# A hybrid recurrent block in fp32 on one core: preparations and inverse moved some input blocks ahead, the recurrence spread over more blocks

## The chip, the core and the metric

The kernel runs on one core of a Trainium2 chip. The metric is the device time of one execution in microseconds (us), as the median of several runs. A core has five engines with instruction queues of their own: TensorE (PE, matrix products), VectorE (DVE), ScalarE (ACT), GpSimd (POOL) and SyncE (SP, which here issues transfers). Each engine works through its queue in order and waits on semaphores for the others.

## The reference

One block over 512 positions of width 1024, batch 1, all in float32:

```python
h = rms_norm(x, norm_mix_g)
proj = h @ w_in + b_in                       # 1024 -> 4864 columns
y_a = rwkv7_branch(proj[:, :1792], ...) @ w_branch_a
y_b = rglru_branch(proj[:, 1792:2304], proj[:, 2304:2816], ...) @ w_branch_b
merged = sigmoid(proj[:, 2816:3840]) * y_a + sigmoid(proj[:, 3840:]) * y_b
x = x + merged @ w_mix_out
x = x + cross_attention(rms_norm(x), rms_norm(mem), w_cq, w_ckv, w_co)
x = x + conv_ffn(rms_norm(x), w_ffn_in, ffn_conv_w, ffn_conv_b, w_ffn_out)
out = rms_norm(x, norm_final_g)
# rwkv7_branch: r, k, v and two low-rank gates are shifted mixes of proj; per head (8 heads of 64) and position
#   sa = S a;  S = S diag(decay) + sa b^T + v k^T;  y = S r
#   then a group norm per head, a bonus sum(r k r_k) v, and a gate
# rglru_branch: xb = causal conv of 4 taps over px; gate_a, gate_x = sigmoid(block products of xb)
#   a = exp(8 gate_a log_sigmoid(lam)); u = xb gate_x sqrt(1 - a^2); h_t = a_t h_(t-1) + u_t; times gelu(py)
```

## The kernel before

**Products.** Channels lie on partitions and positions along the free axis. Each float32 operand is split into a high part (a cast on ACT, `win_h`) and a low part (a subtraction on DVE, `win_l`), and a product is the sum of three: high by high, low by high, high by low. The input projection runs in 38 blocks of 128 output columns. Block i is the PSUM tile `in_ps{i}`; it takes 48 matmuls of 128x256. Blocks 4 to 7 are k, 0 to 3 are r, 8 to 11 are v, 12 and 13 the low-rank inputs, 22 to 37 the merge gates, 14 to 17 px and 18 to 21 py. Weights are loaded by SP through four buffers and split into three pairs of buffers, so that the split of the block number g in `IN_ORDER` needs the end of the block that stands three before it. Three PSUM banks take the blocks' results.

**RWKV-7.** The recurrence is done in 8 chunks of 64 positions. For each pair j of heads come, once its k, r and v blocks are there:

- `prep(j)`: two low-rank products, `psw{j}` and `psa{j}`, and the decays;
- `prep2(j)`: the norm of kk by the product `ss{j}`, and the scaled operands `KBt` (both of its kinds, from kk and from k) and `AK`;
- `scores(j)`: the products `sc{j}`, masked by DVE and ACT into `AK` and `BZ`;
- `bonus_terms(j)`; the bonus products `bo{j}` follow later, DVE multiplies them into `bs{j}`.

Then each chunk's triangular matrix has to be inverted. The 32x32 diagonal blocks go through DRAM (`dM`) into `Nm`, with one block per partition. DVE runs 31 steps of growing size, each a multiplication into `zz` and a reduction into `Zt`, then copies to `Zn`; the result goes back through DRAM (`dZt`, `dZ`) into `ZA` and `BZ`, where products of 32x32, `zh0`, `zo0`, `zh16`, `zo16`, finish the off-diagonal blocks.

Chunk c of the recurrence: `x{c}` (8 products), copied by DVE into `Xs`; `y{c}`, first half; `u{c}` from Xs, copied by ACT and DVE into `UV`; `vr{c+1}`, the next rows of v; `s{c}` from UV; `y{c}`, second half; `kbr{c+1}`, transposes. From s DVE makes `Sn{c}`, then two parts of UV for the next chunk, then two of `SP{c}`. So the chain x, Xs, u, UV, s, Sn, UV, x runs back and forth between PE and DVE.

**RG-LRU.** `px_gates(b)` takes block 14+b: ACT makes `xb{b}`, DVE adds three shifted rows (128x511, 510, 509) and corrects three columns, PE makes `ga{b}` and `gx{b}` from xb. `px_scan(b)` works on pairs of b: exponentials and logarithms on ACT, and on DVE a scan into YB. xb has two buffers, so xb2 takes xb0's, once the scan of xb0 is done. `group_norm(0, jp, ...)` makes `gv0_jp` and `gg0_jp`, in the one PSUM bank that ga0 and gx0 and the like use too.

**Order.** Instructions on DVE, ACT and SP are ordered by the scheduler of the language, by the program's text and priorities. On PE the text table `ORDER` rules: `name` takes all that is left of a tile's products, `name:n` the next n; `Products.arrange` ties each product to the one before it. The other engines' order then follows from what the scheduler expects to be ready. `NSUM` counts, for the sums of squares ahead, how many are made at each block.

Of the kernel before, what the change touches and what calls it, by code (L numbers as in the profile page):

```python
# [41 lines left out]
ORDER = """
in_ps4 in_ps5 in_ps0 in_ps1 in_ps8 in_ps9 psw0 psa0 ss0 in_ps6 in_ps7 in_ps2:6 sc0 in_ps2:12 psw1 psa1 in_ps2:18
ss1 in_ps2 in_ps3 in_ps10:30 sc1 in_ps10 in_ps11 psw2 psa2 ss2 in_ps22 in_ps23 in_ps24:6 sc2 in_ps24 psw3 psa3
ss3 in_ps25 in_ps26 in_ps27:30 sc3 in_ps27 in_ps28 bo0 in_ps29 bo1 in_ps30 bo2 in_ps31 bo3 in_ps32 in_ps33
in_ps34 in_ps35 in_ps36 in_ps37 in_ps14 in_ps15:42 ga0 in_ps15 in_ps16:2 gx0 in_ps16:38 ga1 in_ps16:6 zh0 gx1
in_ps16 in_ps17:4 zo0 zh16 in_ps17:10 zo16 in_ps17:10 vr0 in_ps17:6 x0 y0:8 kbr0 in_ps17:2 u0 vr1 in_ps17:6 s0
y0 kbr1 in_ps17:4 x1 y1:8 in_ps17:2 u1 vr2 in_ps17 s1 y1 kbr2 in_ps18:8 x2 y2:8 in_ps18:4 u2 vr3 s2 y2 kbr3 ga2
in_ps18:2 x3 y3:8 gx2 u3 vr4 s3 y3 kbr4 ga3 x4 y4:8 u4 vr5 gx3 s4 y4 kbr5 in_ps18:6 x5 y5:8 u5 vr6 in_ps18:6 s5
y5 kbr6 in_ps18:2 x6 y6:8 vr7 in_ps18:2 u6 in_ps18:10 s6 y6 kbr7 in_ps18 gv0_0:1 in_ps19:8 x7 y7:8 in_ps19:6 u7  # L50
in_ps19:6 gv0_0 y7 in_ps19:4 gg0_0 in_ps19:20 gv0_1 in_ps19 in_ps20:16 gg0_1 in_ps20 in_ps21 gv1_0 gg1_0 gg1_1
yb_ps0:18 yb_ps1:10 gv1_1 yb_ps1:8 yb_ps0 yb_ps1 yb_ps2 yb_ps3 yb_ps4 yb_ps5 yb_ps6 yb_ps7 ya_ps0 ya_ps1 ya_ps2
ya_ps3 ya_ps4 ya_ps5 ya_ps6 ya_ps7 mix_ps0 mix_ps1 mix_ps2 mix_ps3 mix_ps4 mix_ps5 mix_ps6 mix_ps7 q_ps0_0:32
rxc_ps q_ps0_0 q_ps0_1 q_ps1_0:24 sc_ps0_0 sc_ps0_1 q_ps1_0 q_ps1_1:4 sc_ps0_2 prT_ps0:2 q_ps1_1:8 sc_ps0_3
prT_ps0:2 q_ps1_1:18 prT_ps0 q_ps1_1:10 o_ps0 q_ps1_1 o_ps1 q_ps2_0:4 sc_ps1_0 sc_ps1_1 q_ps2_0:16 sc_ps1_2
prT_ps1:2 sc_ps1_3 prT_ps1:2 q_ps2_0:16 prT_ps1 q_ps2_0:10 o_ps2 q_ps2_0 q_ps2_1:18 o_ps3 q_ps2_1 q_ps3_0:16
sc_ps2_0 sc_ps2_1 q_ps3_0:14 sc_ps2_2 prT_ps2:2 sc_ps2_3 prT_ps2:2 q_ps3_0:16 prT_ps2 q_ps3_0 q_ps3_1:16 o_ps4
q_ps3_1:16 o_ps5 q_ps3_1 co_ps0:16 sc_ps3_0 sc_ps3_1 co_ps0:14 sc_ps3_2 prT_ps3:2 sc_ps3_3 prT_ps3:2 co_ps0:6
co_ps4:10 prT_ps3 co_ps4:10 o_ps6 co_ps4:12 o_ps7 co_ps4:4 co_ps0:6 co_ps4:6 co_ps0 co_ps4 co_ps1
""".split()  # L60


# [17 lines left out]
def hybrid_block_kernel(ctx: ExitStack, tc: tile.TileContext, xT_d, mT_d, pv_d, cst_d, win_d, wk_d, wv_d,  # L80
                        lup_d, gup_d, rga_d, rgx_d, wba_d, wbb_d, wmix_d, wq_d, wo_d, wfi_d, wfo_d, out_d):
    nc = tc.nc
    V, S = nc.vector, nc.scalar
# [76 lines left out]
    def stream(dram, name, between=None, order=None, at=0):  # L160

        for g in order or range(dram.shape[0]):
            with tc.high_priority():
# [9 lines left out]
                wdma.append(ins)
                hi, lo = weight_tiles(name, g, at)
                for o in range(0, 1024, n):
                    casts.append(S.copy(hi[:, o:o + n], raw[:, o:o + n]))  # L176
                    V.tensor_tensor(lo[:, o:o + n], raw[:, o:o + n], hi[:, o:o + n].bitcast(F32), ALU.subtract)  # L177
# [466 lines left out]

    def inproj(i):
        nonlocal last_in
        ps = mm_ps(f"in_ps{i}")
        last_in = dense(ps, uin, lambda kb: (h2[:, 0, kb, :], h2[:, 1, kb, :]), KB, NSUM.get(i, 0))
        return ps

    def evac_shift(ps, blk, out):
# [3 lines left out]
        V.scalar_tensor_tensor(out, ps, omu[:, blk:blk + 1], q, ALU.mult, ALU.add)  # L655
# [113 lines left out]
    for jp in range(2):
        js = (2 * jp, 2 * jp + 1)  # L770
        pks, prs = {}, {}
        for j in js:
            pks[j] = pp.tile([P, T], F32, tag="pk", name=f"pk{j}", bufs=2)
            evac_shift(inproj(4 + j), 4 + j, pks[j])
        for j in js:
            prs[j] = pp.tile([P, T], F32, tag="pr", name=f"pr{j}", bufs=3)
            evac_shift(inproj(j), j, prs[j])
        for j in js:
            evac_shift(inproj(8 + j), 8 + j, vT[:, j, :])
        for j in js:  # L780
            if j == 3:
                for i in IN_REST[:NEARLY]:
                    gate_block(i - 22)
            at, L, Pp = prep(j)
            prep2(j, pks[j], prs[j], at, L, Pp)
            scores(j)
            bonus_terms(j, pks[j], prs[j])
# [838 lines left out]
```

## Time and profile before

| | |
|---|---|
| median of 3 runs | 879.01 us (878.78 to 880.6) |
| the profiled execution | 879.42 us, of which the span of the page is 877.6 |
| PE busy | 855.6 us, 97% of the span |
| DVE, ACT, POOL busy | 679.5, 514.0, 132.5 us |
| mean granted clock of PE | 0.998 |

A page gives the busy time of each engine, and for a group of instructions also the idle time of the engine just before them and what ended it. Since matmuls are pipelined, a matmul's own duration is longer than the distance to the next; delays are best read from starts. The projection blocks end at about 330 us; the preparations lie in 75 to 190, the inverse in 190 to 250, the recurrence in 275 to 330, the group norms and the first products of the branches up to 350.

### The profile page before, as it was taken

The page shows a single profiled execution, that of the slowest core. Times are in us where ns is not written, and L with a number is a line of the kernel's source. Part 1 is how long each engine was busy: PE and PEld are TensorE (multiplying, and loading weights), DVE is VectorE, ACT ScalarE, POOL GpSimd, SP SyncE. Part 2 cuts the span into 40 slices and gives each one's busy share as a digit, 9 for nine tenths or more (in the row PEclk, how much of TensorE's full clock was granted, in tenths as well). Part 3 has the DMA queues.
Part 4 walks back from the last instruction along what each step waited for, and adds up shares of the span by engine and source line. Part 5 has one row for each costly group of instructions (what it writes and reads, how often), then busy time and mean ns, then how long its engine had stood idle before and what let it go on. Part 6 is the DMA issues. An engine that isn't in the chain of part 4 may idle for free.

```text
span 877.6 us, 19313 instructions
## 1 busy us (share of the span) xinstructions
PE 855.6 (97%) x7884; PEld 825.9 (94%) x7884; DVE 679.5 (77%) x1096; ACT 514.0 (59%) x788; POOL 132.5 (15%) x163
## 2 busy tenths in 40 slices
PE   9999989999999999999999999999999999999996
PEld 8889989999997789999999899999999999999996
DVE  6796598877967686685575568799888888999774
ACT  7575676743437687234454356666666566867563
POOL 0102223021101022001122211102111121111100
PEclk9999999999999999999999999999999999999999
DMA  8888799777895479858987858999999999998953
GB/s 284 298 263 220 202 229 232 202 198 242 241 259 138 73 169 265 219 172 223 235 232 168 207 148 201 248 274 276 298 263 293 293 266 305 262 295 212 304 183 96
DMA packets 97576, 201.60 MB, mean 230 GB/s; under 512 B 19600, under 2 KB 30992, under 8 KB 97424
## 3 DMA queue, kind: packets, MB, share of 16 engines
q1 hardware_dynamic: 62240, 118.57, 40.2%
q0 software_dynamic: 25504, 67.38, 37.6%
q10 hardware_dynamic: 9744, 14.42, 4.9%
q8 instruction: 62, 1.02, 0.5%
q14 instruction: 26, 0.21, 0.1%
HBM read 188.54 MB, written 78.12 MB: 304 GB/s over the span
## 4 chain that ended last, share of the span: by engine, by line
PE 74%; DVE 13%; ACT 5%; DMA 4%; issue 3%; DVEq 0%; ACTq 0%; SPq 0%
PE fx_ps L95 14%; PE in_ps L95 13%; PE fyz_ps L95 10%; PE ox_ps L95 7%; PE oyz_ps L95 5%; PE co_ps L95 5%; PE mix_ps L95 4%; PE q_ps L95 4%; PE yb_ps L95 2%; DVE win_l L177 2%; PE v_ps L95 2%; PE o_ps L95 1%; PE k_ps L95 1%; DVE Zt L821 1%; DVE zz L820 1%
## 5 line engine op out<-in xcount | busy, mean ns | idle before, releaser
L95 PE MATMUL in_ps<-hT,win_h 128*128 128x256 f32 x1216 | 214.8, 280 | 2.1 <-DVE pr L655 1.6
L95 PEld LDWEIGHTS in_ps<-hT,win_h 128*128 128x128 f32 x1216 | 185.1, 188 | 6.1 <-DVE pr L655 1.8
L95 PE MATMUL in_ps<-hT,win_l 128*128 128x256 f32 x608 | 170.2, 280 | 1.1 <-DVE win_l L177 1.1
L199 ACT CAST wfi_h<-wfi_r 128x1024 fp32r<-128x1024 f32 x77 | 80.9, 1051 | 69.7 <-PE fyz_ps L95 25.2
L95 PEld LDWEIGHTS in_ps<-hT,win_l 128*128 128x128 f32 x608 | 114.2, 188 | 3.2 <-DVE win_l L177 1.7
L551 POOL DMA_DIRECT2D dS<-in_wfi x66 | 66.8, 1032 | 304.3 <-PE in_ps L95 127.5
L200 DVE TENSOR_TENSOR wfi_l<-wfi_r,wfi_h 128x1024 fp32r<-128x1024 f32 x77 | 94.1, 1222 | 19.8 <-ACT wfi_h L199 19.8
L177 DVE TENSOR_TENSOR win_l<-win_r,win_h 128x1024 fp32r<-128x1024 f32 x38 | 46.3, 1221 | 25.5 <-ACT win_h L176 25.2
L587 POOL DMA_DIRECT2D dOs<-in_wfo x54 | 39.9, 820 | 168.0 <-PE fx_ps L95 45.8
L95 PE MATMUL fx_ps<-hq,wfi_h 128*128 128x256 f32 x352 | 61.2, 276 | 0.0
L95 PE MATMUL fx_ps<-hr,wfi_h 128*128 128x256 f32 x352 | 61.1, 276 | 0.0
L95 PE MATMUL fyz_ps<-hq,wfi_h 128*128 128x256 f32 x352 | 61.1, 276 | 0.0
L95 PE MATMUL ox_ps<-go,wfo_h 128*128 128x256 f32 x352 | 59.9, 276 | 0.0
L176 ACT CAST win_h<-win_r 128x1024 fp32r<-128x1024 f32 x38 | 39.7, 1045 | 34.1 <-PE in_ps L95 31.1
L1436 DVE TENSOR_TENSOR wfo_l<-wfo_r,wfo_h 128x1024 fp32r<-128x1024 f32 (+1 forms) x39 | 47.2, 1213 | 11.6 <-ACT wfo_h L1435 11.6
L1435 ACT CAST wfo_h<-wfo_r 128x1024 fp32r<-128x1024 f32 (+1 forms) x39 | 40.4, 1036 | 25.1 <-DMA wfo_r<-dOs 8.2
L95 PEld LDWEIGHTS fx_ps<-hr,wfi_h 128*128 128x128 f32 x352 | 53.1, 188 | 0.2 <-ACT sn L1371 0.2
L95 PEld LDWEIGHTS fx_ps<-hq,wfi_h 128*128 128x128 f32 x352 | 53.2, 188 | 0.0
L95 PEld LDWEIGHTS fyz_ps<-hq,wfi_h 128*128 128x128 f32 x352 | 53.1, 188 | 0.0
L95 PEld LDWEIGHTS ox_ps<-go,wfo_h 128*128 128x128 f32 x352 | 52.9, 188 | 0.0
L95 PE MATMUL fyz_ps<-hq,wfi_l 128*128 128x256 f32 x176 | 48.7, 277 | 0.6 <-DVE wfi_l L200 0.6
L95 PE MATMUL fx_ps<-hq,wfi_l 128*128 128x256 f32 x176 | 48.6, 276 | 0.0
(392 smaller groups left out, 2337.0 us busy)
## 6 DMA issues: line engine op xcount, KB each, us to landing
dS<-in_wfi POOLq DMA_DIRECT2D x66, 512.0 KB, 8.3
wfi_r<-dS SPq DMA_DIRECT2D x44, 512.0 KB, 7.1
win_r<-in_win SPq DMA_DIRECT2D x38, 512.0 KB, 5.5
...
```

Of the source, the lines that this page charges most:

```text
L95: return self.log(out, nc.tensor.matmul(out, *args, **kw))
L176: casts.append(S.copy(hi[:, o:o + n], raw[:, o:o + n]))
L177: V.tensor_tensor(lo[:, o:o + n], raw[:, o:o + n], hi[:, o:o + n].bitcast(F32), ALU.subtract)
L199: S.copy(hi, raw)
L200: V.tensor_tensor(lo, raw, hi.bitcast(F32), ALU.subtract)
L551: return lambda: nc.gpsimd.dma_start(s(out), src, **kw)
L587: yield lambda k=k, w=w, src=src: nc.gpsimd.dma_start(dO[n, m][:, k * P:(k + w) * P], src, **kw)
L820: V.tensor_tensor(t3, Zt[:, s + 1:, s + 1:], Nm[:, s:s + 1, s + 1:].to_broadcast([P, n, n]), ALU.mult)
L821: V.tensor_reduce(Zt[:, s + 1:, s:s + 1], t3, AX.X, ALU.add)
L1435: S.copy(hi[:, :n], raw[:, :n])
L1436: V.tensor_tensor(lo[:, :n], raw[:, :n], hi[:, :n].bitcast(F32), ALU.subtract)
```

## The change

`NEARLY` goes from 3 to 2, so that two gate blocks instead of three run among the preparations. The loop over two pairs of heads becomes a list of steps, `RWKV_STEPS`: `i4` is the projection block 4, `p0` prep(0), `k0` prep2(0), `f0` scores(0) and bonus_terms(0). `ORDER` is rewritten: psw0 comes four blocks ahead, sc3 90 products earlier, and zh0 likewise, ahead of ga0, gx0 and ga1; the eight chunks, which were packed into blocks 17 to 19, lie in blocks 16 to 21 with fillers of 11 products between their steps; ga0, gx0, ga1, gx1 stand in the first two chunks; the group norms of the first half come in block 21. `ZCASTS` ties eight inverse steps to the low parts number 20 to 27, so that these come first. `NSUM` spreads the 17 sums of squares evenly over blocks 16 to 21. The number of products (7287) is the same.

```diff
-NEARLY = 3
+NEARLY = 2
+RWKV_STEPS = """i4 i5 p0 i0 k0 i1 i8 f0 i9 p1 k1 i6 i7 f1 i2 p2 k2 i3 i10 f2 i11 i22 p3 k3 i23 f3""".split()
+ZCASTS = ((5, 20), (12, 21), (17, 22), (21, 23), (24, 24), (26, 25), (28, 26), (30, 27))
 ORDER = """
-in_ps4 in_ps5 in_ps0 in_ps1 in_ps8 in_ps9 psw0 psa0 ss0 in_ps6 in_ps7 in_ps2:6 sc0 in_ps2:12 psw1 psa1 in_ps2:18
...
+in_ps4 in_ps5 psw0 psa0 in_ps0 in_ps1:6 ss0 in_ps1 in_ps8 sc0 in_ps9 psw1 psa1 ss1 in_ps6 in_ps7 in_ps2:12 sc1 in_ps2
...
+in_ps18:5 u2 vr3 in_ps18:11 s2 y2 kbr3 ga2 in_ps18:11 x3 y3:8 gx2 in_ps18:11 u3 vr4 ga3 in_ps18
...
+                    lows[name, g] = V.tensor_tensor(lo[:, o:o + n], raw[:, o:o + n], hi[:, o:o + n].bitcast(F32),
+                                                    ALU.subtract)
...
-            37: 1, 17: 4, 18: 5, 19: 5, 20: 2, 21: 1}
+            37: 1, 16: 3, 17: 3, 18: 3, 19: 3, 20: 3, 21: 2}
...
+    for step in RWKV_STEPS:
+        what, n = step[0], int(step[1:])
+        if what == "i":
+            rwkv_block(n) if n < 12 else gate_block(n - 22)
+        elif what == "p":
+            Ls[n] = prep(n)
+        elif what == "k":
+            prep2(n, pks[n], prs[n], *Ls[n])
+        else:
+            finish(n)
...
-            if i == 19:
+            if i == 21:
                 for jp in range(2):
                     group_norm(0, jp, rw_ps(f"gv0_{jp}", prg, "rg"), rw_ps(f"gg0_{jp}", prg, "rg"))
...
+    for n, g in ZCASTS:
+        tc.add_manual_dep(steps[n].ins, lows["win", g].ins.name, mybir.DependencyInfo(
+            mybir.DependencyClass.NoSync, mybir.DependencyReason.DATA), reason="order of the casts")
```

Places that matter, as rows of an engine's queue (the line, the operation, the output and inputs, the tile's shape; the numbers behind a name tell tiles apart). On PE before, psw1 stands in block 2, behind the scores sc0:

```order
L95 MATMUL in_ps2_1567<-hT2_0_87,win_h10_1570 128x256
L95 MATMUL in_ps2_1567<-hT2_1_88,win_h10_1570 128x256
L95 MATMUL in_ps2_1567<-hT2_0_87,win_l10_1571 128x256
L95 MATMUL psw1_1361<-pwa0_845,lhi_777 128x512
L95 MATMUL psw1_1361<-pwa0_845,llo0_778 128x512
L95 MATMUL psa1_1362<-pwa1_846,lhi_777 128x512
```

and now behind block 9:

```order
L99 MATMUL in_ps9_1301<-hT2_0_87,win_h7_1304 128x256
L99 MATMUL in_ps9_1301<-hT2_1_88,win_h7_1304 128x256
L99 MATMUL in_ps9_1301<-hT2_0_87,win_l7_1305 128x256
L99 MATMUL psw1_1361<-pwa0_845,lhi_777 128x512
L99 MATMUL psw1_1361<-pwa0_845,llo0_778 128x512
L99 MATMUL psa1_1362<-pwa1_846,lhi_777 128x512
```

The whole of block 9 now lies between sc0 and psw1. On PE at ga2, before and now:

```order
L95 MATMUL s2_3082<-UV2_2994,KBr2_3023 64x64 x8
L95 MATMUL y2_3049<-BZ_757,UV2_2994 64x64 x8
L98 MATMUL kbr3_3100<-cst_76,KBt_758 128x128 x4
L95 MATMUL ga2_4029<-xb2_4023,rg_765 128x512
L95 MATMUL in_ps18_4130<-hT2_0_87,win_h34_4133 128x256
```

```order
L99 MATMUL s2_3082<-UV2_2994,KBr2_3023 64x64 x8
L99 MATMUL y2_3049<-BZ_757,UV2_2994 64x64 x8
L102 MATMUL kbr3_3100<-cst_76,KBt_758 128x128 x4
L99 MATMUL ga2_4032<-xb2_4026,rg_765 128x512
L99 MATMUL in_ps18_4132<-hT2_1_88,win_h34_4135 128x256
```

Nothing moved here; what moved is the work on DVE that ga2 reads. DVE before, from the scan of ga1 to the next SP:

```order
L1029 SCALAR_TENSOR_TENSOR YB_2615<-ga1_3947,xb1_3937 128x512
L1007 SCALAR_TENSOR_TENSOR xb2_4023<-in_ps16_3968,pv_75,xb2_4023 128x510
L1007 SCALAR_TENSOR_TENSOR xb2_4023<-in_ps16_3968,pv_75,xb2_4023 128x509
L949 TENSOR_TENSOR Sn0_2954<-s0_2930,PC_761 128x256
L1009 TENSOR_TENSOR xb2_4023<-xb2_4023,dp_686 128x3
L955 COPY UV1_2918<-Sn0_2954 64x256 x2
L960 TENSOR_TENSOR SP0_2958<-UV1_2918,PC_761 64x256 x2
```

and now:

```order
L182 TENSOR_TENSOR win_l36_4259<-win_r36_4256,win_h36_4258 128x1024
L1043 MEMSET gx1_3948 128x1
L1023 SCALAR_TENSOR_TENSOR xb2_4026<-in_ps16_3968,pv_75,xb2_4026 128x511
L1044 TENSOR_TENSOR xb1_3937<-xb1_3937,gx1_3948 128x512
L965 TENSOR_TENSOR Sn2_3106<-s2_3082,PC_761 128x256
L1045 SCALAR_TENSOR_TENSOR YB_2615<-ga1_3947,xb1_3937 128x512
L969 TENSOR_TENSOR UV3_3070<-Sn2_3106,SP1_3034 64x256 x2
L976 TENSOR_TENSOR SP2_3110<-UV3_3070,PC_761 64x256 x2
L1023 SCALAR_TENSOR_TENSOR xb2_4026<-in_ps16_3968,pv_75,xb2_4026 128x510
L1023 SCALAR_TENSOR_TENSOR xb3_4101<-in_ps17_4043,pv_75,xb3_4101 128x511
L1023 SCALAR_TENSOR_TENSOR xb2_4026<-in_ps16_3968,pv_75,xb2_4026 128x509
L1025 TENSOR_TENSOR xb2_4026<-xb2_4026,dp_686 128x3
```

The last rows of xb2 stood among chunk 0's (Sn0) and now stand behind chunk 2's Sn2, UV3 and SP2.

More of the change, by code (lines that the diff above doesn't have):

```diff
@@ L38 @@
 KVB = 5
+RWKV_STEPS = """i4 i5 p0 i0 k0 i1 i8 f0 i9 p1 k1 i6 i7 f1 i2 p2 k2 i3 i10 f2 i11 i22 p3 k3 i23 f3""".split()
+ZCASTS = ((5, 20), (12, 21), (17, 22), (21, 23), (24, 24), (26, 25), (28, 26), (30, 27))
 IN_ORDER = IN_RWKV + IN_REST
 ORDER = """
-in_ps4 in_ps5 in_ps0 in_ps1 in_ps8 in_ps9 psw0 psa0 ss0 in_ps6 in_ps7 in_ps2:6 sc0 in_ps2:12 psw1 psa1 in_ps2:18
-ss1 in_ps2 in_ps3 in_ps10:30 sc1 in_ps10 in_ps11 psw2 psa2 ss2 in_ps22 in_ps23 in_ps24:6 sc2 in_ps24 psw3 psa3
-ss3 in_ps25 in_ps26 in_ps27:30 sc3 in_ps27 in_ps28 bo0 in_ps29 bo1 in_ps30 bo2 in_ps31 bo3 in_ps32 in_ps33
@@ L46 @@
[L46 to L59, printed above, removed]
+in_ps4 in_ps5 psw0 psa0 in_ps0 in_ps1:6 ss0 in_ps1 in_ps8 sc0 in_ps9 psw1 psa1 ss1 in_ps6 in_ps7 in_ps2:12 sc1 in_ps2
@@ new lines @@
+psw2 psa2 in_ps3:10 ss2 in_ps3 in_ps10 in_ps11:36 sc2 in_ps11 in_ps22 psw3 psa3 ss3 in_ps23 in_ps24 in_ps25:36 sc3 in_ps25
+in_ps26 in_ps27 in_ps28 bo0 in_ps29 bo1 in_ps30 bo2 in_ps31 bo3 in_ps32 in_ps33 in_ps34 in_ps35 in_ps36 in_ps37
+in_ps14 in_ps15:6 zh0 in_ps15:22 zo0 zh16 in_ps15:18 zo16 in_ps15 in_ps16:16 vr0 in_ps16:8
+x0 y0:8 kbr0 ga0 in_ps16:11 u0 vr1 gx0 in_ps16:11 s0 y0 kbr1 ga1 in_ps16
+in_ps17:9 x1 y1:8 gx1 in_ps17:11 u1 vr2 in_ps17:11 s1 y1 kbr2 in_ps17:11 x2 y2:8 in_ps17
+in_ps18:5 u2 vr3 in_ps18:11 s2 y2 kbr3 ga2 in_ps18:11 x3 y3:8 gx2 in_ps18:11 u3 vr4 ga3 in_ps18
@@ new lines @@
+in_ps19:1 s3 y3 kbr4 gx3 in_ps19:11 x4 y4:8 in_ps19:11 u4 vr5 in_ps19:11 s4 y4 kbr5 in_ps19:11 x5 y5:8 in_ps19
+in_ps20:8 u5 vr6 in_ps20:11 s5 y5 kbr6 in_ps20:11 x6 y6:8 in_ps20:11 u6 vr7 in_ps20
+in_ps21:4 s6 y6 kbr7 gv0_0 in_ps21:11 x7 y7:8 gg0_0 in_ps21:11 u7 gv0_1 in_ps21:11 y7 gg0_1 in_ps21
+yb_ps0:18 yb_ps1:18 gv1_0 yb_ps0 yb_ps1 gg1_0
+yb_ps2:12 gv1_1 yb_ps2:20 gg1_1 yb_ps2 yb_ps3 yb_ps4 yb_ps5 yb_ps6 yb_ps7 ya_ps0 ya_ps1 ya_ps2 ya_ps3 ya_ps4 ya_ps5 ya_ps6 ya_ps7 mix_ps0
+mix_ps1 mix_ps2 mix_ps3 mix_ps4 mix_ps5 mix_ps6 mix_ps7 q_ps0_0:32 rxc_ps q_ps0_0 q_ps0_1 q_ps1_0:24 sc_ps0_0
@@ new lines @@
+sc_ps0_1 q_ps1_0 q_ps1_1:4 sc_ps0_2 prT_ps0:2 q_ps1_1:8 sc_ps0_3 prT_ps0:2 q_ps1_1:18 prT_ps0 q_ps1_1:10 o_ps0
+q_ps1_1 o_ps1 q_ps2_0:4 sc_ps1_0 sc_ps1_1 q_ps2_0:16 sc_ps1_2 prT_ps1:2 sc_ps1_3 prT_ps1:2 q_ps2_0:16 prT_ps1
+q_ps2_0:10 o_ps2 q_ps2_0 q_ps2_1:18 o_ps3 q_ps2_1 q_ps3_0:16 sc_ps2_0 sc_ps2_1 q_ps3_0:14 sc_ps2_2 prT_ps2:2
+sc_ps2_3 prT_ps2:2 q_ps3_0:16 prT_ps2 q_ps3_0 q_ps3_1:16 o_ps4 q_ps3_1:16 o_ps5 q_ps3_1 co_ps0:16 sc_ps3_0
+sc_ps3_1 co_ps0:14 sc_ps3_2 prT_ps3:2 sc_ps3_3 prT_ps3:2 co_ps0:6 co_ps4:10 prT_ps3 co_ps4:10 o_ps6 co_ps4:12
@@ L60 @@
+o_ps7 co_ps4:4 co_ps0:6 co_ps4:6 co_ps0 co_ps4 co_ps1
 """.split()
@@ L152, in hybrid_block_kernel @@
     wdma, mdma, casts = [], [], []
+    lows = {}
     OFF = 32
@@ L176, in stream @@
                     casts.append(S.copy(hi[:, o:o + n], raw[:, o:o + n]))
-                    V.tensor_tensor(lo[:, o:o + n], raw[:, o:o + n], hi[:, o:o + n].bitcast(F32), ALU.subtract)
+                    lows[name, g] = V.tensor_tensor(lo[:, o:o + n], raw[:, o:o + n], hi[:, o:o + n].bitcast(F32),
+                                                    ALU.subtract)
                     if between is not None and o == 0:
@@ L767, in gate_block, with rwkv_block, finish @@
         nc.scalar.dma_start(dG[b], sg)
[L769 to L787, printed above, removed]
+    pks, prs, Ls = {}, {}, {}
+    def rwkv_block(i):
+        j = i % 4
+        if i < 4:
+            out = prs[j] = pp.tile([P, T], F32, tag="pr", name=f"pr{j}", bufs=3)
+        elif i < 8:
+            out = pks[j] = pp.tile([P, T], F32, tag="pk", name=f"pk{j}", bufs=2)
+        else:
+            out = vT[:, j, :]
+        evac_shift(inproj(i), i, out)
+    def finish(j):
+        scores(j)
+        bonus_terms(j, pks[j], prs[j])
+    for step in RWKV_STEPS:
[6 more added lines that the diff above has]
+            prep2(n, pks[n], prs[n], *Ls[n])
+        else:
+            finish(n)
     pp_ctx.close()
@@ L801, in hybrid_block_kernel @@
         gate_block(i - 22)
-        if k > 2:
-            bonus(k - 3, bhi[:, k - 3, :], blo[k - 3], last_in)
+        j = k + NEARLY - 6
+        if j >= 0:
+            bonus(j, bhi[:, j, :], blo[j], last_in)
     YB = pq.tile([P, 4, T], F32, tag="YB", name="YB")
@@ L816, in hybrid_block_kernel @@
         V.memset(Zt.rearrange("p a b -> p (a b)")[:, 0:1024:33], 1.0)
+        steps = []
         for s in range(30, -1, -1):
@@ L819, in hybrid_block_kernel @@
             t3 = zz[:, 0:n * n].rearrange("p (a b) -> p a b", b=n)
-            V.tensor_tensor(t3, Zt[:, s + 1:, s + 1:], Nm[:, s:s + 1, s + 1:].to_broadcast([P, n, n]), ALU.mult)
+            steps.append(V.tensor_tensor(t3, Zt[:, s + 1:, s + 1:], Nm[:, s:s + 1, s + 1:].to_broadcast([P, n, n]),
+                                         ALU.mult))
             V.tensor_reduce(Zt[:, s + 1:, s:s + 1], t3, AX.X, ALU.add)
```

## The prediction

> **What bounds the kernel now.** I read the busy shares on the page first, then stretches of the span, then the waits inside the stretches that the change touches.
>
> ```profile
> PE 855.6 (97%) x7884; PEld 825.9 (94%) x7884; DVE 679.5 (77%) x1096; ACT 514.0 (59%) x788; POOL 132.5 (15%) x163
> 112.00:150.00 38.00, 35.03 (x306) 32.60 (x305) 33.91 (x57) 25.66 (x38) 9.28 (x10) 1.00 0.96 239
> 150.00:190.00 40.00, 38.77 (x355) 37.70 (x355) 34.34 (x53) 25.93 (x40) 4.77 (x6) 1.00 0.68 190
> 190.00:255.00 65.00, 63.88 (x548) 62.88 (x547) 51.64 (x87) 23.00 (x29) 8.29 (x9) 1.00 0.88 248
> 255.00:285.00 30.00, 29.05 (x523) 24.55 (x522) 20.38 (x36) 19.01 (x30) 3.72 (x4) 1.00 0.69 170
> 285.00:325.00 40.00, 38.52 (x700) 32.10 (x699) 29.26 (x61) 29.77 (x55) 5.60 (x6) 1.00 0.51 104
> 325.00:350.00 25.00, 24.61 (x202) 23.35 (x202) 17.43 (x27) 17.08 (x26) 5.29 (x6) 1.00 0.96 266
> ```
>
> The columns of a stretch are its length, then busy time of PE, weight load, DVE, ACT and POOL. PE is the bound: the number of its products does not change, so only its holes can be won. The preparations (112 to 190) hold 2.97 + 1.23 = 4.20 us of holes, the 32x32 inverse (190 to 255) 1.12, the recurrence and the group norms (255 to 350) 0.95 + 1.48 + 0.39 = 2.82. The change touches nothing else, so 8.1 us of visible holes is the whole prize, plus what each hole costs in pipelining:
>
> ```profile
> 129.09 0.28 PE L95 MATMUL in_ps<-hT,win_l 128*128 128x256 f32 x1
> 130.95 0.50 PE L95 MATMUL in_ps<-hT,win_h 128*128 128x256 f32 x2 [1.58 <-DVE pr L655]
> 131.29 0.28 PE L95 MATMUL in_ps<-hT,win_l 128*128 128x256 f32 x1
> 131.41 0.39 PE L95 MATMUL in_ps<-hT,win_h 128*128 128x256 f32 x2
> 131.63 0.28 PE L95 MATMUL in_ps<-hT,win_l 128*128 128x256 f32 x1
> ```
>
> Three matmuls take 131.63 - 131.29 = 0.34 us, 0.113 each, though one lasts 0.28. So a hole shown as 1.58 us delays the next start by 130.95 - 129.09 - 0.11 = 1.75: about 0.17 more than it shows. Who is waited for (columns: total us, times, longest), in 100 to 190, in 190 to 255 (one row) and in 255 to 350 (three rows):
>
> ```profile
> PE in_ps L95 <- DVE pr L655: 1.6, 1, 1.6
> PE sc L95 <- ACT kk L694: 1.2, 2, 0.6
> PE sc L95 <- DVE KBt L711: 0.8, 2, 0.6
> PE psa L95 <- ACT BZ L755: 0.3, 1, 0.3
> PE psw L95 <- ACT BZ L755: 0.2, 1, 0.2
> ...
> PE in_ps L95 <- DVE win_l L177: 1.1, 3, 0.5
> ...
> PE s L95 <- DVE UV L933: 1.0, 2, 0.6
> PE zo L95 <- ACT Hs L855: 0.4, 1, 0.4
> PE gv L95 <- DVE gv_l L228: 0.4, 1, 0.4
> ```
>
> **The change, term by term.**
>
> Term 1, the preparations. The named waits are 1.6 + 1.2 + 0.8 + 0.3 + 0.2 = 4.1 us, all of the 4.20. With 0.17 at each of these seven and at about five unnamed ones they are worth 4.2 + 12 x 0.17 = 6.2 us. Now psw0 stands four blocks (in_ps0, 1, 8, 9) ahead of the place that it had, and psw1 after the 48 products of in_ps9 instead of 12 products behind sc0, so the psw and psa waits on scores' evacuation are covered by 48 x 0.113 = 5.4 us. The 1.6 us wait was for DVE, which had two preparations back to back; psw0 and psw1 are now 192 block products apart instead of 114. What stays: sc0 has 90 products after ss0 instead of 102, 1.4 us less cover, where KBt was late already, and on DVE the low part of a weight block (1.2 us, row below) now stands between the two kinds of KBt rows; I keep 0.95 us there, 0.6 for ss0, which now waits for its low part on DVE, 0.35 for sc1 and 0.2 besides: 2.1. The gain is 6.2 - 2.1 = 4.1 us. Bounds: all of it, 6.2, down to 2, if the two largest waits only move.
>
> Term 2, the inverse: DVE's steps from the scores of sc3 to Zn, a way through DRAM, and zh0. A low part of a weight block on DVE, the loads that end that way (their issues and their times to landing), the first zh, and the bonus products:
>
> ```profile
> 244.47 1.22 DVE L177 TENSOR_TENSOR win_l<-win_r,win_h 128x1024 fp32r<-128x1024 f32 x1
> ...
> L842 SPq DMA_DIRECT2D BZ<-dZ x4: 332/647/1332, 252.3 to 255.9; - x4
> DMA to landing us min/median/max: 3.1/4.8/6.2
> ...
> L95 PE MATMUL zh<-ZA,BZ x128: 191/191/212, 264.9 to 269.7; 32*32 32x32 f32 x128
> L728 DVE TENSOR_TENSOR bs<-bo,vT x4: 681/685/693, 197.1 to 219.9; 128x512 f32<-128x512 f32 x4
> ```
>
> sc3 and zh0 both stand about 90 products earlier, so the inverse as a whole moves by 90 x 0.113 = 10.2 us and its length decides. The steps held seven low parts and three bonus products before; now it is seven and four, 0.7 us more. Its last load was issued at 255.9 and landed some 4.8 us later, 260.7, against the first zh at 264.9: a margin of 4.2 us. Of it go the 0.7, and the time of ga0, gx0 and ga1, which PE no longer does ahead of zh0:
>
> ```profile
> 294.55 1.02 PE L95 MATMUL ga<-xb,rg 128*128 128x512 f32 x2
> 295.01 0.80 PE L95 MATMUL in_ps<-hT,win_h 128*128 128x256 f32 x2
> ```
>
> A gate product takes PE 295.01 - 294.55 = 0.46, three of them 1.4. The margin left is 4.2 - 0.7 - 1.4 = 2.1 us: zh0 doesn't wait. The low parts that came late before (1.1 us shown, 3 holes, and a fourth too small for the view, 2.1 by starts) are tied to steps that grow longer towards the end; walking DVE's order step by step I find the low parts of in_ps34 and in_ps35 some 0.7 and 1.4 us late, an estimate: 2.1 again. Term 2 is 0, from -1.5 to +2.
>
> Term 3, the recurrence. Eleven products stand between a chunk's steps, 11 x 0.113 = 1.2 us, so s on UV (1.0) and its like go; zo on Hs and gv stay in some form. By starts the stretch loses 2.82 + 8 x 0.17 = 4.2 us before. What comes in place:
>
> ```profile
> 292.83 0.69 PE L95 MATMUL s<-UV,KBr 128*64 128x64 f32 x16 [0.35 <-DVE UV L933]
> ...
> 282.95 0.15 DVE L1009 TENSOR_TENSOR xb<-xb,dp 128x3 f32<-128x3 f32 x1
> ...
> L1029 DVE TENSOR_TENSOR_SCAN YB<-ga,xb x4: 1215/1225/1226, 275.4 to 319.3; 128x512 f32<-128x512 f32 x4
> ...
> 293.55 0.42 DVE L949 TENSOR_TENSOR Sn<-s,PC 128x256 f32<-128x256 f32 x1
> 293.89 0.74 DVE L1007 SCALAR_TENSOR_TENSOR xb<-in_ps,pv,xb 128x509 f32<-128x509 f32 x1
> 294.55 0.86 DVE L953 TENSOR_TENSOR UV<-Sn,SP 64x256 f32<-64x256 f32 x2
> 295.44 0.87 DVE L960 TENSOR_TENSOR SP<-UV,PC 64x256 f32<-64x256 f32 x2
> 296.35 0.17 DVE L1009 TENSOR_TENSOR xb<-xb,dp 128x3 f32<-128x3 f32 x1
> ```
>
> On PE, s2 y2 kbr3 ga2 follow one another in both kernels, and ga2 comes 294.55 - 292.83 = 1.72 us after s2. ga2 reads xb2. Before, DVE finished xb2 during chunk 0, at 283.1, over 11 us ahead of ga2. Now DVE's order is Sn2, the scan of ga1, two UV3, two SP2, then a row of xb2, one of xb3, the last of xb2, and the short one: Sn2 needs s2, so ga2 waits for all of this. From the rows, start to start: s to Sn 0.72, Sn 0.34, scan 1.23, UV 0.89, SP 0.91, three xb rows 0.66 each, 0.17: 6.24 us after s2. The hole is at least 6.24 - 1.72 = 4.5 us, whatever the first half gains, because both its ends hang on s2; up to 1.2 us more if DVE is behind by one low part (its 1.2 us stands ahead of Sn2) when s2 ends. I take 4.7. After this hole DVE and ACT have caught up, so of the waits further on I keep s5 0.4, x6 1.0 (its UV stands behind YB and a scan on DVE), gg0_0 0.8 and gv0_1 0.45: 2.6. Three more runs of filler cost a switch each, of which no row shows the price alone; I take the 0.17 of a hole's pipelining, rounded up, as an estimate: 0.6. Term 3: 4.7 + 2.6 + 0.6 - 4.2 = +3.7, from +0.9 (4.5 + 0.6 - 4.2: no wait but ga2's, and no backlog) to +4.7 (5.7 + 2.6 + 0.6 - 4.2).
>
> Nothing hides in the queues: the DMA count is unchanged, and SP's loads move with their blocks.
>
> **Sum**: -4.1 + 0 + 3.7 = -0.4 us, 879.0. The profiled execution stands 0.4 above the median of the runs (879.42 against 879.01), so I set the sum against 879.42 and lean by half of that towards the untidy side, since a walk by hand misses small waits more than it invents them: 879.3 us.
>
> **Rivals.**
>
> Slower, the clock falls at ga2. The end of the kernel shows that a pause of PE costs clock, and its start what getting it back costs:
>
> ```profile
> 869.85 0.71 PE L95 MATMUL rs_ps<-t,onesr 128*128 128x128 f32 x4 [0.28 <-ACT t L1477]
> 874.00:875.00 1.00, 0.00 (x0) 0.00 (x0) 0.00 (x0) 0.00 (x0) 0.00 (x0) 0.97 1.02 277
> 875.00:876.00 1.00, 0.00 (x0) 0.00 (x0) 0.00 (x0) 0.00 (x0) 0.00 (x0) 0.50 1.04 294
> 1.07 5.77 PE L95 MATMUL wake<-onesr 128*128 128x512 f32 x17 [1.07 <-DVE Pp L685]
> ```
>
> The last products end at 870.56 and the granted clock goes to 0.50 just before 875, 4.4 us later. The hole at ga2 is 4.5 to 5.7 us, so it reaches that point. The 17 wake matmuls took 5.77 us; at twice 0.113 for 512 columns they would be 3.84, so a cold start loses 1.9 us. The sum becomes -0.4 + 1.9 = +1.5, and with the upper end of term 3 +2.5: 881.4 as the middle. It decides if the hole is longer than the pause that the clock bears; the trace has one fall, at 4.4 us, and the lower end of the hole is just that long, so it may fall short as well. Chance 0.22. The Trainium skill ("TensorE: Matmul & The Clock Gate", Part 1: The HAM clock gate) says that PE's clock halves after one idle window of about 3.4 us that runs freely, and comes back after a busy one; the 4.4 us here agree with it. By that rule a hole of 4.5 us holds a whole window in about a third of its phases (an estimate from that page), and the sum would be +1.5 there and -0.4 in the others.
>
> Slower, the inverse is late. If its length grows by more than the margin of 2.1 us (low parts ahead of steps instead of between), zh0, zo0 and the start of the recurrence wait; the last load took up to 6.2 instead of 4.8, and with two more low parts of 1.2 ahead of Zn it is 1.4 + 2.4 - 2.1 = 1.7 us: 879.0 + 1.7 = 880.7, and with the same lateness again at zh16, 882.4. Chance 0.12.
>
> Slower, the preparations' waits only move (term 1 at its lower end, 2): 879.0 + 2.1 = 881.1. Chance 0.06.
>
> Faster, the small waits vanish. Term 1 at 5.5, the low parts on time through the ties (term 2 at -1.5), term 3 at +2.2 with ga2's hole as its only large wait: -4.8, 874.6. It decides where DVE, at 33.91 of 38 us in the first stretch, keeps up when the two preparations are pulled apart. Chance 0.25.
>
> **How the numbers follow.** 0.2%, 1.8 us, is about what a measurement can tell from no change. My forecast (877.3 to 880.8) has 0.35. Faster 0.25 plus a bit of the forecast's lower edge: 0.29; slower 0.22 + 0.12 + 0.06 less what of these stays inside: 0.36. The range goes to 874.5 below, where the faster case has its middle, and to 883 above, past the middle of the clock case and of the late inverse.
>
> **What would show it.** In the profile after: in 60 to 190 PE's waits sum to some 1.5 us instead of 4.1, the row on pr gone; a row ga on DVE xb of 4 to 6 us, once, the largest of PE's waits there; no wait of zh or only a short one; granted clock under 1.00 behind ga2 in the clock case. The forecast is wrong if DVE finishes xb2 ahead of ga2 (a gain of some 4 us more), or if zh0 waits several microseconds.

## The result: slower by 5 us, and the profile after

The changed kernel takes 884.94 us (median of 6 runs, 884.69 to 886.75) against 879.77 us for the kernel before on the same chip: a ratio of 1.0062, with a 95% interval of 1.0048 to 1.0075. The forecast was 879.3 us, no measurable change, and its range ended at 883.

The same stretches as shown before, of the profile after (length, then busy time of PE, weight load, DVE, ACT and POOL, then PE's granted clock):

```profile
112.00:150.00 38.00, 37.92 (x351) 37.03 (x350) 34.19 (x58) 23.68 (x35) 8.86 (x10) 1.00 1.01 244
150.00:190.00 40.00, 39.79 (x354) 39.05 (x353) 30.63 (x58) 24.02 (x35) 7.94 (x8) 1.00 0.87 240
190.00:255.00 65.00, 61.17 (x595) 60.55 (x595) 46.62 (x64) 20.14 (x25) 6.39 (x8) 0.95 0.89 243
255.00:285.00 30.00, 30.00 (x542) 26.18 (x535) 15.04 (x29) 17.48 (x31) 5.36 (x6) 1.00 0.67 148
285.00:325.00 40.00, 34.02 (x463) 28.83 (x461) 26.22 (x50) 26.51 (x45) 6.98 (x8) 0.91 0.57 123
325.00:350.00 25.00, 22.65 (x303) 20.60 (x304) 17.76 (x33) 14.87 (x25) 3.71 (x4) 1.00 0.81 208
```

From 112 to 190 PE has holes of 0.29 us, where it had 4.20. In return 190 to 255 and 285 to 325 have 3.83 and 5.98 us of holes, and in just these two the granted clock is below 1.00. (325 to 350 has 2.35 us, where it had 0.39: most of it the recurrence's small waits, which now fall there.) The waits of PE between 60 and 372 name the two holes:

```profile
PE ga L99 <- DVE xb L1025: 5.5, 1, 5.5
PE zh L99 <- DMA ZA<-dZt: 3.8, 1, 3.8
PE x L99 <- DVE UV L969: 0.7, 1, 0.7
PE s L99 <- DVE UV L949: 0.7, 1, 0.7
PE gg L99 <- ACT y L328: 0.7, 1, 0.7
PE gv L99 <- ACT UV L948: 0.6, 1, 0.6
```

The rows on pr, win_l, psw and psa are gone. The first row is the hole forecast at ga2; the second, at zh0, was forecast not to be there. Behind each the clock is down for 6.8 us, the last part of the hole included (zh0 from 246, ga2 from 294):

```profile
246.00:248.00 2.00, 0.00 (x0) 0.00 (x0) 0.15 (x1) 0.00 (x0) 0.00 (x0) 0.64 1.18 159
...
250.00:252.00 2.00, 2.00 (x22) 1.94 (x17) 1.51 (x3) 0.58 (x1) 0.00 (x0) 0.50 1.01 403
252.00:254.00 2.00, 2.00 (x13) 2.00 (x13) 1.50 (x3) 0.00 (x0) 0.00 (x0) 0.65 0.79 309
...
294.00:296.00 2.00, 0.00 (x0) 0.00 (x0) 1.99 (x4) 0.00 (x0) 0.00 (x0) 0.59 0.02 6
...
298.00:300.00 2.00, 2.00 (x10) 1.89 (x9) 0.00 (x0) 0.69 (x1) 0.10 (x1) 0.50 0.00 0
300.00:302.00 2.00, 2.00 (x37) 1.71 (x35) 0.42 (x1) 0.00 (x0) 1.06 (x1) 0.70 0.23 11
```

At half clock a block product takes 0.21 us instead of 0.113, though PE reads as fully busy (2.00 of 2.00): this loss shows in no column of busy or idle time, only in the clock and in the count of instructions. DVE's queue at ga2 (its own timeline) is the chain that the prediction walked:

```profile
288.30 1.23 DVE L182 TENSOR_TENSOR win_l<-win_r,win_h 128x1024 fp32r<-128x1024 f32 x1
...
290.85 0.42 DVE L965 TENSOR_TENSOR Sn<-s,PC 128x256 f32<-128x256 f32 x1
291.18 1.22 DVE L1045 TENSOR_TENSOR_SCAN YB<-ga,xb 128x512 f32<-128x512 f32 x1
292.31 0.84 DVE L969 TENSOR_TENSOR UV<-Sn,SP 64x256 f32<-64x256 f32 x2
293.19 0.85 DVE L976 TENSOR_TENSOR SP<-UV,PC 64x256 f32<-64x256 f32 x2
294.06 2.06 DVE L1023 SCALAR_TENSOR_TENSOR xb<-in_ps,pv,xb 128x510 f32<-128x510 f32 x3
296.03 0.15 DVE L1025 TENSOR_TENSOR xb<-xb,dp 128x3 f32<-128x3 f32 x1
```

PE began s2 at 288.81 and would have been at ga2 by 290.4. DVE, one low part and some gate work behind, began Sn2 only at 290.85, and xb2 was done at 296.2.

### The profile page after: what moved, and what is told of

It reads as the page before. It is cut to its first block, busy times and chain, and to the rows that moved or that the text cites. A ratio compares the mean times of both kernels' runs of the same rounds, so it can differ in the third digit from the quotient of the medians.

```text
span 883.3 us, 19296 instructions
## 1 busy us (share of the span) xinstructions
PE 856.9 (97%) x7884; PEld 828.8 (94%) x7884; DVE 677.7 (77%) x1096; ACT 513.5 (58%) x788; POOL 132.6 (15%) x163
## 4 chain that ended last, share of the span: by engine, by line
PE 72%; DVE 13%; ACT 7%; DMA 5%; issue 2%; SPq 1%; ACTq 0%; DVEq 0%
PE fx_ps L99 14%; PE fyz_ps L99 10%; PE in_ps L99 10%; PE ox_ps L99 7%; PE oyz_ps L99 5%; PE co_ps L99 5%; PE mix_ps L99 4%; PE q_ps L99 4%; PE yb_ps L99 2%; PE k_ps L99 2%; DVE win_l L182 2%; PE o_ps L99 1%; PE sc_ps L99 1%; DMA bt<-dBo 1%; PE v_ps L99 1%
## 5 line engine op out<-in xcount | busy, mean ns | idle before, releaser
L99 PE MATMUL in_ps<-hT,win_h 128*128 128x256 f32 x1216 | 219.3, 283 | 0.5 <-DVE hT L459 0.5
L99 PEld LDWEIGHTS in_ps<-hT,win_h 128*128 128x128 f32 x1216 | 187.8, 190 | 5.7 <-issue 2.9
```

The lines of the kernel that those rows point to most:

```text
L99: return self.log(out, nc.tensor.matmul(out, *args, **kw))
```

## The experiments

Each ratio below is to the kernel before, measured beside the run; between runs measured apart the ratios are compared, not the times. The letters name the theories of the expectations.

**One hole at a time, and both.** Four kernels, each an edit of the changed one.

Products of no use in the holes:

```diff
+        if b == 2:
+            for _ in range(16):
+                PE.matmul(psa, onesr, onesr.unsqueeze(1).to_broadcast([P, 4, P]), start=True, stop=True)
         PE.matmul(psa, rg[:, 0, b, :], xb, start=True, stop=True)
...
+        if i0 == 0:
+            for _ in range(12):
+                PE.matmul(psh[0], onesr, onesr.unsqueeze(1).to_broadcast([P, 4, P]), start=True, stop=True)
```

> The changed kernel with 12 products of 128x512 of no use put ahead of zh0 and 16 ahead of ga2, into PSUM tiles that the real products then overwrite: they fill PE's two holes, whose length DVE and the transfers set, and the holes stay as long. Theory A (each hole of PE costs its own length and then a fallen clock besides): the granted clock stays at 1.00, and the time falls by what was lost behind the holes at half clock, 2.2 us at zh0 and 2.3 at ga2, 4.5 in all, to about 880.5. Theory B (the clock's fall costs nothing, since DVE sets the pace there): no change, 885. If the products of no use run longer than the holes, it is slower.

Measured: ratio 1.0034 (1.0021 to 1.0047), 883.61 us, some 2.5 us less than the changed kernel by the ratios: half of what theory A expected. The profile shows why. Behind ga2 the clock stayed at 1.00, but near zh0 it fell all the same, only later, behind a stop of 1.0 us inside zh16:

```profile
256.00:258.00 2.00, 2.00 (x44) 1.96 (x39) 1.13 (x3) 0.58 (x1) 0.00 (x0) 0.68 0.03 10
258.00:260.00 2.00, 2.00 (x12) 2.00 (x11) 0.11 (x1) 0.00 (x0) 0.00 (x0) 0.50 0.00 0
...
294.00:298.00 4.00, 2.13 (x10) 1.46 (x9) 3.91 (x9) 0.78 (x1) 0.00 (x0) 1.00 0.11 43
298.00:302.00 4.00, 4.00 (x48) 3.05 (x48) 1.66 (x4) 0.69 (x1) 1.16 (x1) 1.00 0.15 9
```

From the start of ga2 to the end of the span this kernel takes 585.1 us (882.9 - 297.8) and the changed one 587.1 (883.3 - 296.2). So the fall behind ga2 costs some 2.0 us beside the hole itself, near the 2.3 by starts, and theory B is out. The fall at zh0 wasn't taken away by this kernel.

ga2 and its like later in PE's order:

```diff
-in_ps18:5 u2 vr3 in_ps18:11 s2 y2 kbr3 ga2 in_ps18:11 x3 y3:8 gx2 in_ps18:11 u3 vr4 ga3 in_ps18
-in_ps19:1 s3 y3 kbr4 gx3 in_ps19:11 x4 y4:8 in_ps19:11 u4 vr5 in_ps19:11 s4 y4 kbr5 in_ps19:11 x5 y5:8 in_ps19
+in_ps18:5 u2 vr3 in_ps18:11 s2 y2 kbr3 in_ps18:11 x3 y3:8 in_ps18:11 u3 vr4 ga2 in_ps18
+in_ps19:1 s3 y3 kbr4 gx2 in_ps19:11 x4 y4:8 ga3 in_ps19:11 u4 vr5 gx3 in_ps19:11 s4 y4 kbr5 in_ps19:11 x5 y5:8 in_ps19
```

> The changed kernel with ga2, gx2, ga3 and gx3 each some steps later in PE's order (ga2 behind vr4 instead of behind kbr3), everything else as it is. Theory A (the wait of ga2 on xb2 holds PE 5.7 us and its clock drop 2.3 more): both go, and about 1 us of new waits comes at the later places: 885 - 7 = 878. Rival C (the hole only moves, since DVE is behind by as much at every place of the recurrence): 884 to 885.

Measured: 877.63 us, ratio 0.9965 (0.9952 to 0.9979). By the ratios that is 0.97% or 8.5 us less than the changed kernel. The row of ga on xb is gone, and so is the fall of the clock there; theory A holds, with 1.5 us more than it expected. The hole at zh0 (3.7 us) is as before.

zh0 36 block products later, the three groups behind it closer together:

```diff
-in_ps14 in_ps15:6 zh0 in_ps15:22 zo0 zh16 in_ps15:18 zo16 in_ps15 in_ps16:16 vr0 in_ps16:8
+in_ps14 in_ps15:42 zh0 in_ps15 in_ps16:16 zo0 zh16 in_ps16:8 zo16 vr0
```

> The changed kernel with zh0 36 block products later, zo0, zh16 and zo16 behind it closer together, the recurrence in its place. Theory A (zh0 waits 3.8 us for its operands on their way through DRAM and loses 2.2 more at half clock): 36 x 0.113 = 4.1 us of cover take the wait away: 885 - 5.5 = 879.5. Rival D (the loads come later with PE, since other transfers that PE's progress releases stand in their way): the wait stays, 884 to 885.

Measured: 889.92 us, ratio 1.0106 (1.0093 to 1.0119): slower, which neither theory expected. The wait of zh0 is gone, but PE now stops in the middle of the 64 products of zo16, with nothing that its rows show it waiting for, which the view calls issue (PE's timeline):

```profile
256.93 0.88 PE L99 MATMUL zo<-BZ,Hs 32*32 32x32 f32 x42
261.82 0.80 PE L99 MATMUL zo<-BZ,Hs 32*32 32x32 f32 x22 [4.02 <-issue]
```

The clock is at 0.50 from 261.0 to 271.2, a longer fall than the one that was saved.

Both edits:

> Both moves together: ga2 and its like later, zh0 later. Theory A (the two holes with their clock drops are the whole loss, and hide a gain of 5 to 7 us in the preparations and the inverse): 885 - 12.5 = 872.5, faster than before by 7 us. Theory E (the first half gained little, and what costs is the recurrence spread over six blocks, by switches between small and large products): 879 to 882, no faster than before.

Measured: 881.2 us, ratio 1.0003 (0.9995 to 1.0012). The two edits don't add up: the stops inside zo0 and zo16 (2.3 us, and the clock at 0.50 from 256.4 to 270.1) eat what zh0's place gave. Theory A's number is missed by 9 us, and this run alone can't tell it from theory E; the next two can.

**Where the first half's gain is.** The changed kernel's table up to block 14 and the old one from block 15 on (old `NSUM` from block 16 on, group norms at block 19 again):

```diff
-in_ps14 in_ps15:6 zh0 in_ps15:22 zo0 zh16 in_ps15:18 zo16 in_ps15 in_ps16:16 vr0 in_ps16:8
...
+in_ps14 in_ps15:42 ga0 in_ps15 in_ps16:2 gx0 in_ps16:38 ga1 in_ps16:6 zh0 gx1
...
-            if i == 21:
+            if i == 19:
```

> The changed kernel's preparations and inverse steps (with the tied casts) together with the old order from block 15 on: zh0, gate products, packed recurrence, group norms and sums of squares as before. Theory A (the first half gained 5 us at the preparations and 2 at the inverse): 880 - 7 = 873, since zh0 now has 10 us more cover. Rival E (the first half's gain is eaten later, since DVE or the loads set the pace of the blocks): 877 to 880.

Measured: 873.48 us, ratio 0.9928 (0.9916 to 0.994). Theory A: the first half by itself gains 0.72%, 6.3 us.

**Why zh0 was late.** The inverse's way back goes through SP's queue. In the changed kernel (SP's queue, then the loads of BZ, then those of ZA, which are what zh0 waits for; last, ZA's loads in the kernel before):

```profile
235.19 8.07 SPq L858 DMA_DIRECT2D BZ<-dZ  x3
243.31 1.80 SPq L853 DMA_DIRECT2D ZA<-dZt  x2
...
L858 SPq DMA_DIRECT2D BZ<-dZ x4: 331/1051/5612, 235.2 to 245.2; - x4
...
DMA to landing us min/median/max: 4.6/9.2/9.7
...
L853 SPq DMA_DIRECT2D ZA<-dZt x2: 557/876/1194, 243.3 to 244.6; - x2
...
DMA to landing us min/median/max: 3.8/4.0/4.1
...
L837 SPq DMA_DIRECT2D ZA<-dZt x2: 553/553/553, 254.7 to 255.3; - x2
...
DMA to landing us min/median/max: 3.6/3.8/4.0
```

The longest of BZ's four issues took 5.6 us, and their median landing 9.2, where the trace before had at most 1.3 and 3.8. ZA's loads stand behind three of them in the queue: they land as fast as before, but are issued late. POOL had started transfers of its own at blocks 36 and 37, released by PE's progress. They add up quarters of the ffn weights in DRAM, and it is these sums that `NSUM` counts, not sums of squares:

```profile
228.36 0.77 POOL L557 DMA_DIRECT2D dS<-dS  x1 [4.72 <-PE in_ps L99]
233.81 1.16 POOL L557 DMA_DIRECT2D dS<-in_wfi  x1 [4.67 <-PE in_ps L99]
```

Before, the sums of these blocks were issued by 240.90, and the loads of the way back began at 252.3. With these two sums made later, and ga2 later:

```diff
-            22: 2, 23: 1, 27: 1, 28: 1, 29: 1, 31: 1, 32: 1, 33: 1, 34: 1, 35: 1, 36: 1,
-            37: 1, 16: 3, 17: 3, 18: 3, 19: 3, 20: 3, 21: 2}
+            22: 2, 23: 1, 27: 1, 28: 1, 29: 1, 31: 1, 32: 1, 33: 1, 34: 1, 35: 1, 36: 0,
+            37: 0, 16: 4, 17: 4, 18: 3, 19: 3, 20: 3, 21: 2}
```

> ga2 later, as in that run, and without the sums of ffn weights that POOL starts through DRAM at blocks 36 and 37 (they are made at blocks 16 and 17 instead). In the changed kernel one issue on SP for the inverse's way back takes 5.6 us instead of at most 1.3, just when these transfers run. Theory F (POOL's transfers hold up SP's issue): the issue falls to about 1.3, zh0's wait of 3.7 us and its clock drop go: 877.6 - 5.5 = 872. Rival G (the issue is slow for another reason, its own small packets or the weight loads ahead of it): the issue stays above 4 us and the time at 877 to 878.

Measured: 872.06 us, ratio 0.9908 (0.9895 to 0.9921), the number of theory F. No wait of zh is left and the granted clock is 0.999 over the span. The largest waits of PE from 60 to 372, and the issues of the way back:

```profile
PE gv L99 <- ACT UV L948: 1.0, 1, 1.0
PE x L99 <- DVE UV L969: 0.8, 1, 0.8
...
L858 SPq DMA_DIRECT2D BZ<-dZ x4: 331/584/2393, 233.5 to 238.9; - x4
```

The longest issue is 2.4 us: not the 1.3 expected, but enough. The kernel with this edit alone completes the square:

> The changed kernel with one edit: the sums of blocks 36 and 37 made at blocks 16 and 17; ga2 stays where the change put it. With the run that has both edits (872.1), the one with ga2 alone (877.6) and the changed kernel (885) this completes a square. Theory A (two holes that add up, each with its clock drop): zh0's hole goes, ga2's stays, 885 - 5.5 = 879.5, that is no difference to before. Rival L (the holes hang together, ga2's becomes longer once zh0's is gone): 882 or more.

Measured: 879.96 us, ratio 0.9991 (0.9982 to 0.9999). zh0's wait on the transfer is gone (a stop of 0.5 us on issue is left, and the longest issue on SP is still 3.6 us), ga2's stays at 5.6 with its fall of the clock. In ratios to the kernel before: 1.0062 with neither edit, 0.9965 with ga2's, 0.9991 with the sums', 0.9908 with both. ga2's edit takes 0.97% or 0.83%, the sums' edit 0.71% or 0.57%: they add up to within 0.14%, about half the width of an interval, as theory A has it.

**zh0 later without closer groups**, and the ties of the casts:

```diff
+in_ps14 in_ps15:42 zh0 in_ps15 in_ps16:16 zo0 zh16 in_ps16:18 zo16 in_ps16 in_ps17:4 vr0 in_ps17:8 x0 y0:8 kbr0 ga0
+in_ps17:10 u0 vr1 gx0 in_ps17:10 s0 y0 kbr1 ga1 in_ps17:10 x1 y1:8 gx1 in_ps17 in_ps18:4 u1 vr2 in_ps18:10 s1
...
```

> ga2 later, and zh0 36 block products later with all the old distances kept between zh0, zo0, zh16, zo16, vr0 and x0 (in the run with zh0 later they were cut, and PE stood 4 us inside zo16 with nothing that the profile shows it waiting for); the recurrence's fillers shrink from 11 to 10 and 9. Theory H (the stop inside zo16 came from small products packed too closely for the supply of instructions): no stop, no wait of zh0, clock at 1.00 there: 877.6 - 5.5 = 872, less about 1 for the thinner fillers. Rival I (the stop comes whenever zh0 is later): 880 or more.

Measured: 885.41 us, ratio 1.0069 (1.0056 to 1.0083). Rival I, and more: the stop inside zo16 is still there (2.3 us), so close packing alone doesn't make it, and a new hole of 5.6 us appears where a block waits for DVE's rows of xb to free its PSUM bank. Moving zh0 is no cure here.

```diff
-    for n, g in ZCASTS:
+    for n, g in ():
```

> ga2 later, and the ties between the inverse's steps and the low parts of the weights left out. Theory J (the ties only set the same order that the scheduler finds anyway): within 1 us of 877.6. Theory K (they hold the low parts ahead of the long steps): PE waits 2 us on low parts as before the change, but the inverse may end earlier and zh0's wait fall: 877 to 880.

Measured: 877.82 us, ratio 0.9965 (0.9951 to 0.9979), the same ratio as with the ties: theory J, the ties change nothing measurable in the time (zh0's wait is 2.9 us here instead of 3.7).

**The stops without a visible cause.** Two kernels move POOL's sums out of their way. First, in the kernel with ga2 and zh0 both later:

```diff
-            37: 1, 16: 3, 17: 3, 18: 3, 19: 3, 20: 3, 21: 2}
+            37: 1, 17: 4, 18: 4, 19: 4, 20: 3, 21: 2}
```

> The run with ga2 and zh0 both later (881.2), in which PE stood 2 us inside zo0 and zo16 with nothing in the profile that it waits for, with the three sums of block 16 made at blocks 17, 18 and 19. Theory M (PE's supply of instructions is held up by POOL's transfers, and the many small products of zh and zo use it up quickly): the stops inside zo go, and with them the clock drop behind them: 881 - 5 = 876. Theory N (the stops come from the small products alone): 880 to 882 as before.

Measured: 877.63 us, ratio 0.997 (0.9958 to 0.9983), 3.3 per mille less. The stops inside zo shrink from 2.3 to 1.0 us and don't go, and the clock still falls there; between M and N this is a half answer. Then, in the kernel with the first half alone:

```diff
-            37: 1, 17: 4, 18: 5, 19: 5, 20: 2, 21: 1}
+            37: 1, 18: 6, 19: 6, 20: 3, 21: 2}
```

> The first half of the change with the old recurrence (873.5), in which PE stood 1.5 us inside y0 without a visible reason and the clock fell behind it, with the four sums of block 17 made at blocks 18 to 21. Theory M: the stop inside y0 and the clock drop go, 873.5 - 3 = 870.5. Theory N: the stop stays, 873 to 874. If the later blocks take the sums badly, a stop comes there instead.

Measured: 878.49 us, ratio 0.9971 (0.9959 to 0.9983), 0.43% slower than with the sums at block 17, by the ratios. The stop inside y0 (1.5 us) and its fall of the clock are gone, as theory M has it. The profile shows a price 120 us later, where products of w_mix_out now wait and the clock falls; but the profiled execution, 881.84 us, is the slowest of twelve (875.1 to 881.8), so this wait needn't be the price in all of them:

```profile
PE mix_ps L97 <- ACT mg L1105: 2.1, 1, 2.1
...
390.00:400.00 10.00, 7.43 (x36) 6.93 (x37) 5.85 (x8) 3.28 (x5) 0.70 (x1) 0.66 0.39 125
```

What PE waits for in these stops is the supply of its instructions. The DMA view has a queue of instruction packets; here it is for the run with zh0 later, first over the whole span, then in the stop of 4.0 us (257.8 to 261.8):

```profile
q8 instruction: 62, 1.02, 0.5%
...
q8 instruction: 1, 0.02, 2.4%
```

62 packets of 16 KB stand against 15,836 instructions of PE (loads of weights, products and a few others), some 255 to a packet, so 256 to a full one. The runs have ten stops on issue of 0.3 to 4.0 us between 240 and 300. At each of them the count of PE's instructions is 193 to 195 above a multiple of 256, and PE goes on 0.9 to 1.6 us after such a packet has landed. In the stop of 4.0 us the packet moved from 259.05 to 260.58, and PE went on at 261.82. What makes a packet late, POOL's transfers or the small products that use up the instructions quickly, these runs don't separate: moving the sums shortened some stops and took one away, as theory M has it.

## Why the prediction was wrong, by its own steps

**Term 1, the preparations: right.** The last product of the scores stood at 184.8 before and at 169.5 after. Of the 15.3 us, 10.2 are the 90 products fewer ahead of it; 5.1 are gained, where 4.1 were forecast and 2 to 6.2 allowed.

**Term 2, the inverse: failed, and this is the step that made the forecast wrong.** It was taken as 0; by starts it is -2.1 for the low parts, 3.8 for zh0's wait and 2.2 for the clock behind it, +3.9. Two of its parts were off. The low parts, forecast late by 2.1 us, aren't late at all. And "zh0 doesn't wait" stood on a margin of 2.1 us, of which three readings were wrong. The first is the gate products: 0.46 us each came from the start of a row that groups two matmuls. Read over a longer stretch, from the profile after, it is twice that:

```profile
305.18 1.12 PE L99 MATMUL ga<-xb,rg 128*128 128x512 f32 x2
305.75 0.68 PE L99 MATMUL in_ps<-hT,win_l 128*128 128x256 f32 x1
306.26 0.40 PE L99 MATMUL in_ps<-hT,win_h 128*128 128x256 f32 x2
```

From 305.18 to 306.26 PE does one gate product and one block product of 0.113: 0.97. Three gate products are 2.9, not 1.4. The second is the load: zh0 reads ZA, not the last load of BZ, and the 4.8 us to landing is the median of dZ's loads and stores together. ZA's last load was issued at 255.3 and landed within 4.0, by 259.3, so zh0 at 264.9 had 5.6 us to spare, not 4.2. The third and largest is the way through DRAM, which was taken to be as long as before. It had been priced at a time when POOL's transfers were done, and moving the inverse moved it among them.

With these the wait comes out. From the last product of the scores to zh0 PE's own work fell from 80.1 us (264.9 - 184.8) to 75.1 (244.6 - 169.5): 5.0 less, the 2.1 of the low parts and the 2.9 of the gate products. From the same product to ZA's landing the inverse grew from 74.5 (259.3 - 184.8) to 78.9 (248.4 - 169.5): 4.4 more, although DVE reached the store of Zt 1.5 sooner (58.3 after that product instead of 59.8); the way back is 5.9 longer. 5.6 - 5.0 - 4.4 = -3.8, the wait measured.

The rival "the inverse is late" named this event, but priced it by low parts ahead of Zn, 1.7 us, which play no part, and gave it 0.12. Without this wait the kernel stands where the forecast had it: the run with the sums' edit alone has a ratio of 0.9991. That is in part luck, since there the 2.3 us of clock at ga2 that the sum left out meet the 2.1 of low parts that it didn't count as won.

**Term 3, the recurrence: right in kind, its size at the upper end.** ga2's wait was forecast at 4.5 to 5.7, taken as 4.7; it is 5.5 by the view and 5.7 by starts. The backlog of one low part ahead of Sn2 is what was named as the reason for the upper end. The waits kept further on (s5, x6, gg0_0, gv0_1, 2.6 in all) came as 2.7.

**The clock: the rival came true, twice.** The hole at ga2 cost 2.3 us at half clock, against 1.9 forecast in the rival, and zh0's 2.2. The prediction kept the hole in its sum and the clock outside it, as a case of 0.22; and it priced the rivals one at a time, 881 to 882, though nothing keeps them apart. The chance was too low because the rival asked for a pause as long as the 4.4 us at the kernel's end. The Trainium skill ("TensorE: Matmul & The Clock Gate", Part 1: The HAM clock gate) says that an idle window of about 3.4 us halves the clock. The length agrees with these traces: after the start-up and before the last product, every stretch at half clock in the runs here lasts a whole multiple of 3.41 us (up to four, 13.65, with both later). That the window has to be idle does not agree. The first row is the window that ended with the fall at zh0, the second the stretch at half clock behind it, the third the window that ended with the fall at ga2 (profile after):

```profile
243.16:246.57 3.41, 1.45 (x13) 1.25 (x12) 1.22 (x1) 1.73 (x2) 0.00 (x0) 1.00 0.86 150
246.57:253.40 6.83, 4.97 (x78) 4.90 (x79) 2.88 (x5) 0.58 (x1) 0.00 (x0) 0.50 1.02 320
290.95:294.36 3.41, 0.00 (x0) 0.00 (x0) 3.32 (x7) 1.15 (x2) 0.00 (x0) 1.00 0.78 275
```

At ga2 PE was idle for the whole window. At zh0 it worked for 1.45 of the 3.41 us, and the clock fell 2.0 us after its last product.

**All terms.** Sum as measured: -5.1 for the preparations, -2.1 for the low parts, 3.8 + 2.2 at zh0, 5.7 + 2.3 at ga2, 2.7 + 0.6 - 4.2 for the rest of the recurrence, the 0.6 unmeasured: +5.9, against 5.2 by the medians. (One slip of arithmetic plays no part: half of 0.4 added to 879.0 is 879.2, not 879.3.)

The change is a gain of some 8 us (5.1 + 2.1 + 0.9) that two holes hide, and both have small remedies: with ga2 some steps later and two weight sums some blocks later it runs at 872.06 us, 0.92% (0.79 to 1.05) under the kernel before.
